# Hybrid trunk: weight sums in place, a second decay tile, and unit inputs added on VectorE

## The chip, the cores and the metric

The kernel runs on one core of one Trainium2 chip. The metric is the device time of one execution in microseconds (us). Engines are named as the profile does: PE is TensorE's matmul, PEld its weight load, DVE is VectorE, ACT ScalarE, POOL GpSimd, and SP the SyncE queue, from which nearly all DMA transfers are issued.

## The reference

One layer over 2048 positions with 1024 channels in f32. A normalised input goes through one projection `w_in`; its columns feed a short gated convolution (group A) and a chunked state-space scan (group B). The two results are concatenated, projected by `w_out` and added to `x`; then follow a norm, a squared-ReLU MLP, and a last norm. Cut to its skeleton:

```python
h = rmsnorm(x, norm_mix_w)
u_b, u_c, u_h, z, xbc, dt_raw = split(h @ w_in)
y_a = u_b * causal_dwconv(u_c * u_h, short_conv_w)
y_b = ssd_mixer(z, xbc, dt_raw, ...)        # conv, silu, chunked scan, gate, norm
x = x + concatenate([y_a, y_b]) @ w_out
h = rmsnorm(x, norm_mlp_w)
x = x + square(relu(h @ w_up)) @ w_down
out = rmsnorm(x, final_norm_w)
```

In the scan, each chunk of a head has a decay matrix: the exponential of differences of running sums, with what lies above the diagonal set to zero. It weighs the scores of the chunk before they are multiplied with its inputs.

## The kernel before

Positions are held in four blocks of 512 (`TB`), channels on the 128 partitions. Every large product is made of f32 operands that are split in two: `hi` is a cast to fp32r on ScalarE and `lo` the rest, subtracted on VectorE (`split_w`, L101 to L105, for weights, with lines L103 and L104; `settle`, L390 and L391, for inputs). A product is then three matmuls of 128x128 by 128x512: hi by hi, hi by lo, lo by hi (L315 to L317, in `chain`).

Most of the large products use seven products in place of eight. The chain `b11, t1, t2, b21, t3, b22, t4` takes a pair of weight blocks `r0`, `r1` and two sums of them, `s12` and `s34`. `combine` makes these: it yields the split of `r0`, then of `s12`, then of `s34`, then of half of `r1`. Raw weights lie in three `wraw` buffers, the sums in `sumtile`, a pool `us` of two buffers. With `kept` the sums are also stored and read back by the second half. With `kept == "none"`, which pair 3 of the output projection sets (`sums_d["o4"]`), all sums are made first and nothing is stored, and its first split comes one step later.

The output projection (`Output`) works in two parts. Eight pairs (`pair`) treat group A's half of `w_out` by the seven products, and store partial sums to DRAM (`x1_d`). The scan's second part, chunks 20 to 31, runs beside them: `hook` steps the generator `scan.run`, whose chunk is a `front` (transposes, decay, copies of the chunk's input) and a `back` (state, outputs, gate). The tiles of the second part come from the pool `sp2` with one buffer each, but for `bc` with two. The decay tile `dec` holds 8 rows of running sums, broadcast by a DMA (L1380). ScalarE makes eight Relus in place of it (L1431), one cast for the states (`xtok`, L1432) and one exponential (L1433); VectorE masks it (L1439), and the matmuls `yd` (L1456) read it. `run` issues the loads of chunk n + 1 (`load`) after the second step of `back(n)`.

Then come 32 plain units (`unit`, n = 32 to 63) for group B's half of `w_out`. A unit is 24 matmuls (L1687 to L1689) into one PSUM bank. The bank is first filled by ScalarE with the block of `x` that the residual adds: `seed`, L1658, from the tile `xr`, which has one buffer and is loaded by L1665. The first matmul of a unit then accumulates onto the seed. VectorE adds the partial sum `xt` (three buffers, load L1653) to the bank (the evict, L1691), the result goes back to `x1_d` (store, L1692), and for the first half of the positions its square is taken for the MLP's norm (`square`). Banks are taken in turn from `k0`, `k1` and `k2`. So the bank of unit n is the bank of unit n + 3, and the load of `xt` of unit n + 3 waits for the store of unit n.

From unit 48 on, the MLP's first input places are made beside the units: `prepare(0, ...)` scales the stored rows (`first`, `stay`, `nb`; L439), sums them (`sub`, L234), and `settle` splits them (L390, L391). `sums_of(0, 0)` makes the first weights of `w_up` ahead. After unit 63, PE goes into the MLP (`half`), whose `prepare(1, ...)` squares the stored rows of the second half of the positions (loads `lx`, squares L418).

The order of the instructions on each engine is not that of the Python text. A scheduler places them by its own estimates of when operands are there, within what the pools, the semaphores and `tc.issue_after` allow; the text sets what may precede what, and which buffer waits for which.

## Time and profile before

| what | value |
|---|---|
| median of 3 timed runs | 2607.75 us (2606.67 to 2608.23) |
| profiled execution, its own time | 2605.26 us |
| span of its instructions | 2603.5 us |
| mean granted TensorE clock | 0.996 |
| PE busy | 2570.4 us (99%), 12027 matmuls |
| PEld busy | 2110.9 us (81%) |
| DVE busy | 1928.4 us (74%), 2619 instructions |
| ACT busy | 1438.0 us (55%), 2199 instructions |
| POOL busy | 74.7 us (3%) |
| DMA | 552.84 MB, mean 212 GB/s |

The 2605.26 us are the device time of the one execution that the profile shows; the span is the part of it between its first and last instruction. All times of single instructions come from this execution, counted from the span's start. Matmuls are pipelined: each is shown with 0.39 us, but the next starts 0.23 us after it, so the rows of PE overlap. In a row of a timeline, the numbers are start and duration, and the bracket at its end is the time in which the engine stood idle before it and what released it. In a list of waits stand the total, the count and the longest.

The parts of the span that the change concerns, all read from the timeline: the second part of the scan runs from about 985 us, its last chunk ends at about 1235; unit 32 starts at 1156, unit 48 at 1263, unit 63 at 1347, and the MLP's first product at 1353.

### The profile page before, as it was taken

The numbers are of one execution on the slowest core, as the hardware profiler recorded it, in microseconds if no ns is written. First come the engines' busy times: TensorE is split into PE (matmuls) and PEld (weight loads), VectorE is DVE, ScalarE is ACT, GpSimd is POOL, SyncE is SP. The second block draws the span as 40 slices with busy tenths as digits, with TensorE's granted clock in tenths as the row PEclk, the third lists the DMA queues.
The fourth block names the chain that finished last, engine by engine and source line by source line (L and its number), as shares of the span: only waits on it lengthen the run. The fifth ranks groups of instructions, "written<-read, shape, count | busy, mean of one in ns | idle before, by whom it ended". The sixth has DMA issues, their size and how long they took to land.

```text
span 2603.5 us, 33796 instructions
## 1 busy us (share of the span) xinstructions
PE 2570.4 (99%) x12027; PEld 2110.9 (81%) x12027; DVE 1928.4 (74%) x2619; ACT 1438.0 (55%) x2199; POOL 74.7 (3%) x99
## 2 busy tenths in 40 slices
PE   9999999999999999999999999999999999999998
PEld 7888878788888887778878888888888888888887
DVE  7877776878787777888777765644448887888985
ACT  6554345876576666766346555655556444444443
POOL 2110010000000000000000000000000000000001
PEclk9999999999999999999999999999999999999999
DMA  4555665766655567878876785865557664665762
GB/s 168 181 190 185 220 237 184 234 194 197 195 179 186 171 231 250 261 232 278 261 234 230 270 316 221 294 211 194 194 190 260 187 183 150 213 211 179 239 208 76
DMA packets 258856, 552.84 MB, mean 212 GB/s; under 512 B 26976, under 2 KB 94336, under 8 KB 258688
## 3 DMA queue, kind: packets, MB, share of 16 engines
q1 hardware_dynamic: 258112, 549.78, 63.1%
q8 instruction: 94, 1.54, 0.2%
q10 hardware_dynamic: 576, 0.92, 0.1%
q14 instruction: 74, 0.61, 0.1%
HBM read 364.20 MB, written 186.40 MB: 211 GB/s over the span
## 4 chain that ended last, share of the span: by engine, by line
PE 78%; DVE 7%; DMA 7%; ACT 4%; issue 3%; SPq 0%; POOL 0%; POOLq 0%; DVEq 0%; ACTq 0%
PE px L315 14%; PE px L316 14%; PE px L317 14%; PE py L315 7%; PE py L316 7%; PE py L317 7%; PE pw L315 3%; PE pw L317 3%; PE pw L316 3%; DMA dec<-rd_d 1%; DMA xr<-x 1%; DVE ul L391 1%; PE yd L1456 1%; ACT dec L1431 1%; DVE wlo L104 1%
## 5 line engine op out<-in xcount | busy, mean ns | idle before, releaser
L315 PE MATMUL px<-uh,whi 128*128 128x512 f32 x1800 | 706.4, 393 | 8.8 <-DVE xt L1691 4.1
L317 PE MATMUL px<-uh,wlo 128*128 128x512 f32 x1800 | 702.4, 390 | 0.0
L316 PE MATMUL px<-ul,whi 128*128 128x512 f32 x1800 | 701.9, 390 | 0.0
L315 PEld LDWEIGHTS px<-uh,whi 128*128 128x128 f32 x1800 | 338.3, 188 | 86.9 <-DVE xt L1691 4.5
L317 PEld LDWEIGHTS px<-uh,wlo 128*128 128x128 f32 x1800 | 338.3, 188 | 73.1 <-issue 2.2
L316 PEld LDWEIGHTS px<-ul,whi 128*128 128x128 f32 x1800 | 338.4, 188 | 69.0 <-issue 0.3
L104 DVE TENSOR_TENSOR wlo<-wraw,whi 128x512 fp32r<-128x512 f32 (+1 forms) x213 | 217.3, 1020 | 201.3 <-ACT whi L103 199.0
L315 PE MATMUL py<-uh,whi 128*128 128x512 f32 x900 | 352.4, 392 | 1.6 <-ACT facc L1625 1.1
L317 PE MATMUL py<-uh,wlo 128*128 128x512 f32 x900 | 350.9, 390 | 0.0
L316 PE MATMUL py<-ul,whi 128*128 128x512 f32 x900 | 350.5, 389 | 0.0
L103 ACT CAST whi<-s 128x1024 fp32r<-128x1024 f32 x226 | 236.3, 1046 | 192.3 <-PE py L316 88.1
L104 DVE TENSOR_TENSOR wlo<-s,whi 128x1024 fp32r<-128x1024 f32 x226 | 275.2, 1218 | 88.8 <-ACT whi L103 87.7
L103 ACT CAST whi<-wraw 128x1024 fp32r<-128x1024 f32 (+1 forms) x214 | 190.2, 889 | 254.4 <-PE px L316 208.5
L315 PEld LDWEIGHTS py<-uh,whi 128*128 128x128 f32 x900 | 169.0, 188 | 40.2 <-issue 2.1
L316 PEld LDWEIGHTS py<-ul,whi 128*128 128x128 f32 x900 | 169.0, 188 | 35.3 <-issue 0.8
L317 PEld LDWEIGHTS py<-uh,wlo 128*128 128x128 f32 x900 | 169.0, 188 | 35.3 <-issue 0.2
L315 PE MATMUL pw<-uh,whi 128*128 128x512 f32 x450 | 176.3, 392 | 0.0
L317 PE MATMUL pw<-uh,wlo 128*128 128x512 f32 x450 | 175.3, 390 | 0.0
L316 PE MATMUL pw<-ul,whi 128*128 128x512 f32 x450 | 175.1, 389 | 0.0
L391 DVE TENSOR_TENSOR ul<-rh,uh 128x1024 fp32r<-128x1024 f32 (+1 forms) x128 | 138.7, 1088 | 32.1 <-ACT uh L390 32.1
L390 ACT CAST uh<-rh 128x1024 fp32r<-128x1024 f32 (+1 forms) x128 | 119.8, 941 | 73.0 <-PE py L317 59.4
L322 ACT COPY pw<-px 128x512 f32<-128x512 f32 x115 | 65.8, 573 | 125.9 <-PE px L317 125.5
(272 smaller groups left out, 3686.8 us busy)
## 6 DMA issues: line engine op xcount, KB each, us to landing
hid_d<-e SPq DMA_DIRECT2D x96, 512.0 KB, 3.3
rh<-hid_d SPq DMA_DIRECT2D x96, 512.0 KB, 4.6
wraw<-w_in SPq DMA_DIRECT2D x68, 512.0 KB, 4.2
wraw<-w_down SPq DMA_DIRECT2D x104, 256.0 KB, 3.5
wraw<-w_up SPq DMA_DIRECT2D x48, 512.0 KB, 3.7
dec<-rd_d SPq DMA_DIRECT2D x32, 512.0 KB, 5.3
wraw<-w_out SPq DMA_DIRECT2D x32, 512.0 KB, 5.3
sums_d<-s SPq DMA_DIRECT2D x32, 512.0 KB, 5.0
```

The costliest lines, as they stand in the source:

```text
L103: nc.scalar.copy(hi, raw)
L104: split["last"] = eng.tensor_tensor(out=lo, in0=raw, in1=hi.bitcast(F32), op=ALU.subtract)
L315: nc.tensor.matmul(p, hi, h[0], start=not seeded and k == 0, stop=False, **kw)
L316: nc.tensor.matmul(p, hi, h[1], start=False, stop=False, **kw)
L317: nc.tensor.matmul(p, lo, h[0], start=False, stop=(k == len(g) - 1), **kw)
L322: nc.scalar.copy(pm[gi]["w"], pm[gi]["x"])
L390: nc.scalar.copy(p[i][0], t)
L391: nc.vector.tensor_tensor(out=p[i][1], in0=t, in1=p[i][0].bitcast(F32), op=ALU.subtract)
L1431: nc.scalar.activation(dec[:, i], dec[:, i], AF.Relu, bias=t["a"][:, i : i + 1], scale=-1.0)
L1456: nc.tensor.matmul(yd[(i % 2) * 64 : (i % 2) * 64 + 64, (i // 2) * L : (i // 2 + 1) * L], byhead(t["xdt"])[:, i, :], t["dec"][:, i % 2 * 4 ...
```

## The change

It has four parts.

*Sums in place.* `Seven.inplace`: with it, `combine` writes `s34` over the raw tile `r0`, which has been split by then, instead of into a tile of `us`. It is set for the output projection and for the MLP's first weights (until unit 63 is done). The pool `us` of the output projection falls to one buffer; the tile `rn` of `norm` shares it. Pair 3 loses its path of its own (`"none"`) and takes the normal order of splits.

*Decay tiles in two buffers.* `sp2` is opened with two buffers, and all its tiles but `dec` (and `bc`) are held to one. `run` issues the loads of chunk n + 1 one step earlier. On SyncE, this is the load of a `dec` tile near the end of the pairs (`y`: the gate; `xd`, `bc`, `eb`: other tiles of the chunk; `rn`, `ry`: for scaling group B's rows; `x1`: partial sums). Before:

```order
L1401 DMA y_10254<-sz_d1_108 128x4x128
L1508 DMA rn_10379<-rn_d1_0_113 128x512
L1378 DMA xd_10329<-xs_d1_106 128x4x128
L1508 DMA rn_10379<-rn_d1_1_114 128x512
L98 DMA wraw_10426<-w_out 128x1024
L1665 DMA xr_10422<-x 128x512
L1653 DMA xt_10363<-x1_d0_77 128x512
L98 DMA wraw_10503<-w_out 128x1024
L1562 DMA ry_10371<-yn_d0_109 128x2x512
L1627 DMA x1_d2_79<-facc_10274 128x512
L1380 DMA dec_10331<-rd_d3_126 128x1024
```

and now:

```order
L1379 DMA bc_10300<-xs_d1_106 128x128
L1397 DMA eb_10132<-rd_d3_126 64x512 x2
L1379 DMA bc_10300<-xs_d1_106 128x128
L1383 DMA dec_10305<-rd_d3_126 128x1024
L1633 DMA x1_d3_80<-xt_10004 128x512
L1477 DMA yn_d1_110<-y_10049 128x4x128
L98 DMA wraw_10176<-w_out 128x1024
L1633 DMA x1_d2_79<-facc_10152 128x512
L1404 DMA y_10247<-sz_d1_108 128x4x128
L1381 DMA xd_10303<-xs_d1_106 128x4x128
L1678 DMA xr_10415<-x 128x512
```

The load has moved from behind the chunk's `y`, `xd`, `rn`, two raw weights and others to ahead of them, right behind `bc`.

*Seeds up to unit 47.* The tiles `xr` of units 35 to 47 lie in places of `ul3` that are not in use then, with four buffers, and for units 34 to 45 `seed(n)` also issues the load of unit n + 2. The copies on ScalarE stay.

*Units 48 to 63 without seeds.* ScalarE copies nothing. The unit's first matmul starts the bank, and VectorE adds `xr` to `xt` (L1695 of the changed kernel) right after the evict of the unit before, before its own evict (L1712 there). `xr` comes from a pool `late` with two buffers, loaded two units ahead. On VectorE this is the stretch around the evict of unit 57 (`wlo`: split of a weight; `ul`: split of an input; `s12`, `s34`: sums of the first `w_up` pair). Before, from a sum for the MLP's input to that evict, the last row:

```order
L234 TENSOR_TENSOR nb_11867<-nb_11868,first_11866 128x512
L391 TENSOR_TENSOR ul2_11929<-nb_11868,uh2_11928 128x1024
L234 TENSOR_TENSOR nb_11869<-nb_11867 128x512
L1691 TENSOR_TENSOR xt_11748<-pm_11768,xt_11748 128x512
L104 TENSOR_TENSOR wlo_11847<-wraw_11844,whi_11846 128x1024
L391 TENSOR_TENSOR ul3_11933<-nb_11869,uh3_11932 128x512
L269 TENSOR_TENSOR s12_12057<-wraw_11971 128x512
L234 TENSOR_TENSOR s34_12095<-wraw_11969,wraw_11971 128x512
L234 TENSOR_TENSOR s12_12057<-s12_12057,wraw_11969 128x512
L234 TENSOR_TENSOR s34_12095<-wraw_11969,s12_12057 128x512
L1691 TENSOR_TENSOR xt_11794<-pm_11808,xt_11794 128x512
```

and now, the adds of units 57 and 58 among them, the evict of unit 57 in the seventh row:

```order
L1695 TENSOR_TENSOR xt_11786<-xt_11786,xr_11749 128x512
L442 SCALAR_TENSOR_TENSOR nb_11859<-nb_11859,cv_169,facc_10478 128x512
L236 TENSOR_TENSOR first_11858<-nb_11861,first_11858 128x512
L236 TENSOR_TENSOR nb_11860<-nb_11860,nb_11861 128x512
L236 TENSOR_TENSOR nb_11859<-nb_11860,first_11858 128x512
L271 TENSOR_TENSOR s12_12049<-wraw_11963 128x512
L1712 TENSOR_TENSOR xt_11786<-pm_11803,xt_11786 128x512
L1695 TENSOR_TENSOR xt_11834<-xt_11834,xr_11789 128x512
L236 TENSOR_TENSOR nb_11861<-nb_11859 128x512
L393 TENSOR_TENSOR ul2_11921<-nb_11860,uh2_11920 128x1024
L393 TENSOR_TENSOR ul3_11925<-nb_11861,uh3_11924 128x512
L236 TENSOR_TENSOR s12_12049<-s12_12049,wraw_11961 128x512
```

Two splits of inputs and four sums that stood ahead of the evict of unit 57 now stand behind it, and adds stand ahead of and behind it. The end of the units, from the evict of unit 62 to that of unit 63, before:

```order
L1691 TENSOR_TENSOR xt_12009<-pm_12023,xt_12009 128x512
L104 TENSOR_TENSOR wlo_12100<-s34_12095,whi_12099 128x1024
L269 TENSOR_TENSOR s12_12233<-wraw_12175 128x512
L391 TENSOR_TENSOR ul1_12130<-stay_11585,uh1_12129 128x1024
L234 TENSOR_TENSOR s12_12233<-s12_12233,wraw_12173 128x512
L391 TENSOR_TENSOR ul1_12134<-stay_11679,uh1_12133 128x1024
L391 TENSOR_TENSOR ul1_12138<-stay_11773,uh1_12137 128x1024
L1691 TENSOR_TENSOR xt_12065<-pm_12079,xt_12065 128x512
```

and now:

```order
L1712 TENSOR_TENSOR xt_12001<-pm_12018,xt_12001 128x512
L1695 TENSOR_TENSOR xt_12057<-xt_12057,xr_12004 128x512
L104 TENSOR_TENSOR wlo_12091<-wraw_11961,whi_12090 128x1024
L393 TENSOR_TENSOR ul1_12122<-stay_11577,uh1_12121 128x1024
L393 TENSOR_TENSOR ul1_12126<-stay_11671,uh1_12125 128x1024
L393 TENSOR_TENSOR ul1_12130<-stay_11765,uh1_12129 128x1024
L1712 TENSOR_TENSOR xt_12057<-pm_12072,xt_12057 128x512
```

Between the two evicts stands the add of unit 63, and the two sums of the next weights are gone from there. PE's order is the same as before throughout.

*Loads for the second half.* `prepare(1, ...)` may issue its `lx` loads only behind the store of unit 63.

The diff, cut to its core:

```diff
         def combine(self, r0, r1, kept=None):
...
-            s34 = self.sumtile("s34")[:, 0 : 2 * w]
+            s34 = r0 if self.inplace else self.sumtile("s34")[:, 0 : 2 * w]
...
-        def prepare(self, h, src, base, accs=None):
+        def prepare(self, h, src, base, accs=None, begin=None):
...
-                                nc.sync.dma_start(ts[-1], src[h * NBB + bb][:, j : j + 2])
+                                with tc.issue_after(begin.ins) if begin else nullcontext():
+                                    nc.sync.dma_start(ts[-1], src[h * NBB + bb][:, j : j + 2])
...
-            t["dec"] = self.tile([HG, L], "dec")
+            t["dec"] = self.tile([HG, L], "dec", self.bufs)
...
                 next(back)
+                if self.bufs > 1:
+                    self.load(n + 1)
                 yield
                 next(back)
-                self.load(n + 1)
+                if self.bufs == 1:
+                    self.load(n + 1)
...
             if p == 3:
                 proj.new = [{} for _ in range(4)]
-                sums_d["o4"] = "none"
...
                 pm = self.pm[n] = psum("mm", "pm")
-                nc.scalar.copy(pm, self.res.pop(n))
-                self.origin(n + 1)
+                if n < 48:
+                    nc.scalar.copy(pm, self.res.pop(n))
+                if n < 48:
+                    self.origin(n + 1)
+                if 33 < n < 46:
+                    self.origin(n + 2)
...
-                t = self.res[n] = self.small("xr")
+                if n < 35 or n == 48:
+                    t = self.small("xr")
+                elif n > 48:
+                    t = self.late.tile([P, TB], F32, tag="xr", name="xr", bufs=2)
+                else:
+                    t = uh.tile([P, TB], F32, tag="ul3", name="xr", bufs=4)
+                self.res[n] = t
                 nc.sync.dma_start(t, x[b, :, d])
...
+            fresh = n >= 48
+            if fresh:
+                with tc.issue_after(self.evicted.ins):
+                    nc.vector.tensor_tensor(out=self.xt[n], in0=self.xt[n], in1=self.res.pop(n), op=ALU.add)
+                if n == 48:
+                    self.origin(49)
+                self.origin(n + 2)
...
+                nc.tensor.matmul(pm, w, hi, start=fresh and j == 0, stop=False, **kw)
...
-            proj.sumtile = lambda name: os.tile([P, 1024], F32, tag="us", name=name, bufs=2)
-            scan.open(c2, "sp2", 1)
+            proj.sumtile = lambda name: os.tile([P, 1024], F32, tag="us", name=name, bufs=1)
+            scan.open(c2, "sp2", 2)
...
-        ws = mlp.half(0, ws, mlp.prepare(1, x1_d, C_NMLP))
+        ws = mlp.half(0, ws, mlp.prepare(1, x1_d, C_NMLP, begin=proj_out.stored))
```

More of the change, by code (lines that the diff above doesn't have):

```diff
@@ L216, in trunk @@
     class Seven:
+        inplace = False
         def __init__(self):
@@ L1369, in load @@
             if (g, c) == (0, 0) or n == self.begin:
-                dd = self.tile([4, NC * 16], "dd")
+                dd = self.tile([4, NC * 16], "dd", 1)
                 nc.sync.dma_start(dd, dt_d[b])
@@ L1399, in load_gate @@
             b, g, c, h, ts, r0 = self.place(n)
-            y = self.got[n]["y"] = self.tile([4, L], "y")
+            y = self.got[n]["y"] = self.tile([4, L], "y", 1)
             nc.sync.dma_start(y, sz_d[h][:, 4 * g : 4 * g + 4, ts])
@@ L1586, in open @@
             proj.fresh = self.raw
+            proj.inplace = True
         def raw(self, name):
@@ L1635, in after @@
                     proj.got = proj.fetch(0)
-                if p == 3:
-                    if name == "t1":
-                        next(ahead)
-                    if name != "b11":
-                        proj.refresh(name)
+                if p == 3 and name != "b11":
+                    proj.refresh(name)
                 hook(7 * p + n)
@@ L1686, in unit @@
                 w, v = whi[:, k, :], wlo[:, k, :]
-                nc.tensor.matmul(pm, w, hi, start=False, stop=False, skip_group_check=True)
-                nc.tensor.matmul(pm, w, lo, start=False, stop=False, skip_group_check=True)
-                nc.tensor.matmul(pm, v, hi, start=False, stop=(j == KD - 1), skip_group_check=True)
+                kw = dict(skip_group_check=not fresh)
+                nc.tensor.matmul(pm, w, hi, start=fresh and j == 0, stop=False, **kw)
+                nc.tensor.matmul(pm, w, lo, start=False, stop=False, **kw)
+                nc.tensor.matmul(pm, v, hi, start=False, stop=(j == KD - 1), **kw)
             t = self.xt.pop(n)
-            nc.vector.tensor_tensor(out=t, in0=pm, in1=t, op=ALU.add)
-            nc.sync.dma_start(x1_d[b][:, d], t)
+            self.evicted = nc.vector.tensor_tensor(out=t, in0=pm, in1=t, op=ALU.add)
+            self.stored = nc.sync.dma_start(x1_d[b][:, d], t)
             if i and b < NBB:
@@ L1774, in trunk @@
         mlp.up = proj_out.xp
-        mlp.us = c4.enter_context(tc.tile_pool(name="us", bufs=1, side="right", reuse_waits="tile"))
+        mlp.inplace = True
         c7 = c4.enter_context(ExitStack())
+        proj_out.late = c7.enter_context(tc.tile_pool(name="late", bufs=1, side="right", reuse_waits="tile"))
+        mlp.sumtile = lambda name: proj_out.late.tile([P, 1024], F32, tag="us", name=name, bufs=1)
         stay = c7.enter_context(tc.tile_pool(name="stay", bufs=1, side="right", reuse_waits="tile"))
@@ L1799, in trunk @@
         c7.close()
+        mlp.us = c4.enter_context(tc.tile_pool(name="us", bufs=1, side="right", reuse_waits="tile"))
+        mlp.inplace = False
+        del mlp.sumtile
     turns.update(mm=itertools.cycle(("k0", "k1", "k2", "k4")), mw=itertools.cycle(("k3", "k5")), fresh=("k3", "k5"))
```

4 lines of the change are left out of this document (2 added, 2 removed).

## The prediction

> **What bounds the kernel now.** I read the page first, then the busy time by stretch, then TensorE's waits in the stretch that the change touches, then the timelines around the longest of them. PE's instructions stand in the same order in both kernels, and the other queues in nearly the same up to about 985 us, so the time before that I take as given. The stretch from 985 to 1365 us (second scan part beside the w_out pairs, its end beside the units, the units alone, the start of the MLP); the columns are busy time and instructions of PE, PEld, DVE, ACT and POOL, then PE's clock, the DMA share and GB/s:
>
> ```profile
> 985.00:1365.00 380.00, 365.38 (x1815) 296.70 (x1814) 298.57 (x420) 221.10 (x400) 0.00 (x0) 1.00 0.79 252
> ```
>
> PE is busy for 365.4 of 380 us, and its matmul count does not change: the change can win no more than the 14.6 us in which PE stands still there, and little beside. VectorE is the second engine, at 79%. TensorE's waits from 855 to 1375 us, total, times, longest:
>
> ```profile
> PE px L315 <- DVE xt L1691: 4.1, 1, 4.1
> PE pn L1486 <- ACT xtok L1416: 2.5, 1, 2.5
> PE pm L1687 <- ACT pm L1658: 2.5, 4, 1.3
> PE st L118 <- ACT xtok L1432: 2.4, 2, 1.5
> PE py L315 <- ACT facc L1625: 1.1, 1, 1.1
> PE px L315 <- DVE xt L1622: 0.9, 1, 0.9
> PE st L119 <- DVE stmp L1434: 0.9, 2, 0.5
> PE ptx L1411 <- DMA xd<-xs_d: 0.7, 1, 0.7
> ```
>
> The releasers are ACT and DVE, but these are late themselves. ScalarE's own waits from 855 to 1240 us say for what:
>
> ```profile
> ACT pm L1658 <- DMA xr<-x: 24.3, 7, 8.6
> ...
> ACT dec L1431 <- DMA dec<-rd_d: 16.6, 10, 5.3
> ```
>
> Two loads into single buffers, the unit seeds xr and the decay rows dec, hold ScalarE's queue, and PE pays behind it. The places on PE that the sum uses:
>
> ```profile
> 1005.48 0.50 PE L118 MATMUL st<-xtok,btok 128*128 128x512 f32 x1 [1.50 <-ACT xtok L1432]
> ...
> 1159.27 0.43 PE L1486 MATMUL pn<-ssq,ones_r 128*32 128x128 f32 x8 [2.52 <-ACT xtok L1416]
> ...
> 1206.50 0.50 PE L1687 MATMUL pm<-uh,whi 128*128 128x512 f32 x1 [1.32 <-ACT pm L1658]
> ...
> 1330.18 0.50 PE L1687 MATMUL pm<-uh,whi 128*128 128x512 f32 x1 [0.42 <-ACT pm L1658]
> ...
> 1359.03 0.69 PE L315 MATMUL px<-uh,whi 128*128 128x512 f32 x1 [4.06 <-DVE xt L1691]
> ```
>
> **Decay tiles in two buffers.** SyncE's load and ScalarE's next Relu at the costlier chunk (the later SyncE rows are used below):
>
> ```profile
> 1147.14 0.33 SPq L1380 DMA_DIRECT2D dec<-rd_d  x1
> ...
> 1309.31 0.32 SPq L1653 DMA_DIRECT2D xt<-x_d  x1
> ...
> 1348.23 0.32 SPq L1653 DMA_DIRECT2D xt<-x_d  x1
> ```
>
> ```profile
> 1154.05 1.29 ACT L1431 ACTIVATE dec<-dec,dd 128x128 f32<-128x128 f32 x4 [5.29 <-DMA dec<-rd_d]
> ```
>
> The load goes out only when the yd matmuls have read the last tile, and ScalarE gets it nearly 7 us later; the copies that PE waits for are queued behind the eight Relus. With a second buffer the load stands 12 rows earlier on SyncE at this place, ahead of gate, xd and rn loads. On it hang 1.5 us of PE at 1005, 2.5 at 1159, and the longer of the two waits on L1434, 0.5, which comes by the same chain through VectorE: 4.5 in all. Next late are xd and eb, which keep one buffer. Bounds of what they take back: 0, if they keep ahead, and all 4.5, if they land as late as dec did. The trace has xd as PE's last wait once, for 0.7; I take 1.0, near that row, so 3.5 net.
>
> **Seeds of units 33 to 47.** Their xr tiles now lie in unused places and load up to two units ahead. The 1.3 us at 1206 are the longest wait on L1658, and ScalarE's backlog there comes from its stops on xr, the longest of 8.6 us. Bounds 0 and 1.3; I take 1.3.
>
> **Units 48 to 63: copies go, adds come.** Sixteen seed copies leave ScalarE, and with them the other three waits on L1658, 2.5 - 1.3 = 1.2 us, since the first matmul of these units starts the bank itself. Sixteen adds xt += xr come to VectorE, each right behind the evict of the unit before. The nearest row is the evict, the same addition with one operand in PSUM:
>
> ```profile
> L1691 DVE TENSOR_TENSOR xt<-pm,xt 128x512 f32<-128x512 f32 x18 | 12.3, 686 | 5.0 <-DMA xt<-x_d 5.0
> ```
>
> ```profile
> 1278.63 3.35 DVE L189 RECIPROCAL facc<-facc 128x512 f32<-128x512 f32 x1 [3.34 <-ACT facc L188]
> ...
> 1313.76 0.71 DVE L1691 TENSOR_TENSOR xt<-pm,xt 128x512 f32<-128x512 f32 x1
> ...
> 1318.79 0.75 DVE L439 SCALAR_TENSOR_TENSOR nb<-nb,cv,facc 128x512 f32<-128x512 f32 x1 [2.52 <-DMA nb<-x_d]
> ...
> 1326.66 1.28 DVE L1691 TENSOR_TENSOR xt<-pm,xt 128x512 f32<-128x512 f32 x2
> ...
> 1358.29 0.69 DVE L1691 TENSOR_TENSOR xt<-pm,xt 128x512 f32<-128x512 f32 x1
> ```
>
> Two in a row take 1.28 us, so each puts back what follows by 0.60: 16 x 0.60 = 9.6 us of VectorE. Is there room? A unit's bank is needed again three units later. The first evict at 1326.66 is unit 57's; it ends at 1327.3, and unit 60, which takes that bank, began at 1330.2: slack 2.8 us. Eight adds (50 to 57) put evict 57 back by 4.8. Against that the first reciprocal no longer waits 3.34: its sqrt stood on ScalarE behind a seed copy that waited for xr, and now follows the sum of squares directly. And the order moves one split of 1024, one of 512 and four sums of 512 elements from ahead of evict 57 to behind it, about 1.1 + 0.6 + 4 x 0.6 = 4.1. So it moves by 4.8 - 3.3 - 4.1 = -2.6 us, and by up to 2.5 more if the idle time before 1318.79 fills. Under that cover the adds cost nothing; without it (neither gap closes, the order as before) evict 57 would be 4.8 later, and PE would lose 4.8 - 2.8 = 2.0.
>
> The add also waits for its xt and xr. Queued behind it on VectorE are the scalings and sums for the MLP's input and the evict of its own unit; ScalarE's casts of nb, the store, and PE by its bank wait for those. On SyncE the xr load two units on waits for the add, with the unit's store behind it. The sixteen xt loads of L1653:
>
> ```profile
> DMA to landing us min/median/max: 2.8/4.8/6.3
> ```
>
> The load at 1309.31 is unit 56's, the tightest of units 51 to 58; evict 55, behind which add 56 stands, began 4.45 us later, at 1313.76. Add 56 would thus wait between 0 and 1.9 us, 0.4 by the median. With evicts earlier by a like amount the stores are too, so I count this as zero.
>
> One rule bears on these loads: the Trainium skill, "DMA: Bandwidth & Descriptors", section "Anatomy of one DMA — SWDGE (gpsimd) path", fits a transfer as about 2.0 us plus its bytes at 436 GB/s (on another issue path than this), which I turn into an estimate of 2.6 us for the 256 KB of xt. The trace disagrees, with a median of 4.8 at this DMA share; by the page no add would wait, the residual of the next part would be nil, and the sum 0.8 better.
>
> **Into the MLP.** The longest stall, seen on ScalarE:
>
> ```profile
> 1345.20 0.59 ACT L1658 COPY pm<-xr 128x512 f32<-128x512 f32 x1 [2.53 <-DMA xr<-x]
> ```
>
> PE's 4.1 us at 1359 wait for unit 63's evict at 1358.29. That stood behind a VectorE queue that began late, since ScalarE's casts of the MLP's first places came after this copy, held 2.5 us for xr. The copy is gone, and so are the squares for half 1, whose lx loads wait for the last store now. New is add 63: from the landing of xt 63 the add, one split and three subtractions stand ahead of evict 63, 0.6 + 4 x 1.1 = 5.0 us. With its load at 1348.23, landing at 1351.0 to 1354.5, evict 63 would start at 1356.0 to 1359.5, hardly better than 1358.29. But that load follows, by stores and three buffers, from evict 60 and that from evict 57. Evict 60 is the one that waited 5.0 for xt (the L1691 row), and evict 57 moves 2.6 to 5.1 us up; with 3 us on the chain evict 63 starts at 1353.0 to 1356.5. PE began to wait at 1359.0 - 4.1 = 1354.9. So with evict and restart of 0.75 the residual lies between 0 and 2.4, more (3.3) if the chain gains only 2; I take 0.8. Gain 3.3.
>
> **In one sentence each.** With s34 in the first raw tile and one us buffer, a raw tile is held until its last split, and the next pair's second load starts a few us later; a pair's 84 matmuls outlast these loads several times, so it costs 0 (up to 1 us if a first product comes late). Pair 3 without its extra path: PE's waits on L1625 and L1622, 1.1 + 0.9 = 2.0, hang on a backlog of casts that stays; between 0 and 2.0, I take 0.4. The squares for half 1 have all of half 0 to finish in, cost 0.
>
> **The sum.** 3.5 + 1.3 + 1.2 + 3.3 + 0.4 = 9.7 us won. The profiled execution took 2605.26 us (span 2603.5), 2.5 under the median of the three timed runs, 2607.75, whose lowest is 2606.67. It would go to 2595.6, and on the median's basis 2607.75 - 9.7 = 2598.0. With each term at its good end (4.5 + 1.3 + 1.2 + 4.1 + 2.0 = 13.1) it is 2594.6; with each at its bad end (0 + 0 + 1.2 + 0.8 + 0 - 1.0 = 1.0) 2606.8.
>
> **Rivals.** *The add chain keeps the last stall.* Add 63 waits for its load as reckoned with nothing earlier, and PE still stands 4 us before the MLP. For it: the same three xt buffers and the same way from store to load. Against it: three causes of the lateness go. Gain 9.7 - 3.3 = 6.4, 2601.3; chance 0.13. *xd or eb takes the place of dec.* For it: a DMA share of 0.79 and one buffer each; against it the single wait of 0.7. Gain 9.7 - 3.5 = 6.2, 2601.5; chance 0.13. *The adds are paid in full.* If VectorE sets the end of the units, 9.6 come back and 0.1 is left: 2607.6, no change; against it stand the 5.0, 3.3 and 2.5 us in which VectorE idles; chance 0.06. The Trainium skill, "VectorE: DVE Perf Modes", section "Rules for kernel authors", speaks for this one: it advises to keep the count of chained operations low, and the change raises it by 16. *Slower.* The adds wait for xt at each of units 50 to 57, w on average. With the slack of 2.8 + 2.6 = 5.4 used up, PE pays 8w - 5.4; the kernel loses when that exceeds 9.7, w over 1.9, and by over 0.2% from w = 2.6. At 2.8 it is 17.0, so 7.3 slower, 2615.1. The tightest load bounds its wait at 1.9, against this; chance 0.06.
>
> **Numbers.** Forecast 0.62, rivals as given. About 0.2%, 5.2 us, is what a measurement of this kernel can tell from no change: faster means under 2602.5, which takes the forecast and some 0.16 of the first two rivals, 0.78; the rest of them and the third make 0.16; slower 0.06. The range runs from the good end, 2594.5, to 2604.5, the first two rivals and 3 us for their terms at bad ends; what lies beyond, the last two rivals and tails, is about 0.15.
>
> **What would show it.** In the profile after: no wait of ScalarE for dec over 1 us from chunk 21 on, no PE idle at st and pn; no wait of PE on L1658 after unit 33; evict 57 at least 4 us ahead of unit 60's start; PE idle before the MLP's second product under 2 us. I am wrong if the adds wait over 2 us each for xt, if xd takes the place of dec, or if new PE idle stands in the pairs, on a weight split that comes late.

## The result and the profile after

In its first runs the change gained more than forecast. The changed kernel took 2595.07 us as the median of four runs (2589.88 to 2597.05) beside 2607.99 for the kernel before (2606.67 to 2609.54), a ratio of 0.9947 [0.993, 0.9964]: 12.9 us by the medians, 9.4 to 18.3 by the interval, against a forecast gain of 9.7. On two other chips the same pair gave 0.9956 [0.9943, 0.9969] and 0.9965 [0.9952, 0.9978], or 11.8 and 9.0 us. Over all runs on record, 65 of the kernel before and 15 of the changed one, the medians are 2607.75 and 2597.06 us, 10.7 us apart, so the forecast of 9.7 is not far from the gain.

The profiled execution took 2595.14 us (span 2593.4, clock 0.997). The stretch from 985 to 1365 us, columns as before:

```profile
985.00:1365.00 380.00, 373.89 (x1864) 306.17 (x1863) 311.96 (x439) 218.87 (x388) 0.00 (x0) 1.00 0.79 255
```

PE stands still for 6.1 us there, where it stood still for 14.6. Its waits from 855 to 1375 us:

```profile
PE px L317 <- DVE xt L1628: 2.3, 1, 2.3
PE ptx L1414 <- DMA xd<-xs_d: 2.2, 1, 2.2
PE px L317 <- ACT s L807: 1.0, 1, 1.0
PE pm L1708 <- ACT uh L1583: 0.9, 1, 0.9
PE st L118 <- ACT xtok L1435: 0.7, 1, 0.7
PE px L317 <- DVE eb L810: 0.5, 1, 0.5
PE st L119 <- DVE stmp L1437: 0.3, 1, 0.3
```

The waits on the unit seeds, on `pn` and on unit 63's evict are gone. Two that were short have grown: the one for xd in place of 0.7, and the one in pair 3 (L1628) in place of 0.9. ScalarE still waits for dec from 855 to 1240 us:

```profile
ACT dec L1434 <- DMA dec<-rd_d: 13.8, 5, 4.2
```

The second buffer took 2.8 of 16.6 us from it, and the longest is 4.2 in place of 5.3. The two grown waits on PE:

```profile
1010.15 0.33 PE L1414 MATMUL ptx<-ident,xd 128*128 128x128 f32 x1 [2.16 <-DMA xd<-xs_d]
...
1062.88 0.50 PE L317 MATMUL px<-uh,whi 128*128 128x512 f32 x1 [2.32 <-DVE xt L1628]
...
1064.31 0.63 PE L319 MATMUL px<-uh,wlo 128*128 128x512 f32 x1
1064.73 0.63 PE L317 MATMUL px<-uh,whi 128*128 128x512 f32 x1
```

At 1010 xd is the last to land, which is the rival from the prediction, at this one place. And dec is late still: ScalarE waits for it 4.1 us at 1172 and 3.2 at 1214, where the prediction had no wait over 1 us from chunk 21 on as a sign of being right. Behind the wait at 1063 something else shows. From 1064.3 matmuls last 0.63 us and start 0.42 apart, where 0.23 is usual. The same stretch as a window, with the clock in the third column from the end:

```profile
1063.90:1067.20 3.30, 3.30 (x9) 2.61 (x8) 2.65 (x4) 3.27 (x4) 0.00 (x0) 0.51 0.89 290
```

The clock was granted at half over these 3.3 us. The kernel before has the same behind its longest stall, the 4.06 us at 1359:

```profile
1359.00:1362.40 3.40, 3.37 (x8) 2.72 (x9) 3.40 (x5) 0.00 (x0) 0.00 (x0) 0.53 0.56 141
```

```profile
1359.52 0.63 PE L316 MATMUL px<-ul,whi 128*128 128x512 f32 x1
1359.95 0.63 PE L317 MATMUL px<-uh,wlo 128*128 128x512 f32 x1
...
1362.79 0.40 PE L315 MATMUL px<-uh,whi 128*128 128x512 f32 x1
1363.03 0.40 PE L316 MATMUL px<-ul,whi 128*128 128x512 f32 x1
```

Eight matmuls at 0.43 us in place of 0.23 are 1.6 us that no idle time shows, and the prediction put them at nothing. In the profile after, the way into the MLP is clean, with PE busy throughout and the clock at 1.00:

```profile
1345.00:1360.00 15.00, 15.00 (x67) 12.09 (x66) 12.63 (x16) 9.52 (x11) 0.00 (x0) 1.00 0.68 228
```

**Place by place.** All but 197 of PE's 12027 matmuls stand at the same place of its order in both profiles, so each can be paired with itself. The 197 lie between the marks of the table (at 1002 to 1017, 1060 to 1084, 1159 to 1180 and 1354 to 1367 us). There PE's order did change, against what was said of it ahead of the result: ahead of `pn`, for one, stand five matmuls of unit 32 where two stood before. The difference of a matmul's two starts says how far ahead the changed kernel is there; the growth from one mark to the next (before's time) is the gain of that stretch. Three profiles of the changed kernel (the two others are the controls f0 after and f0 again below), in us:

| stretch | what lies there | forecast | after | f0 after | f0 again |
|---|---|---|---|---|---|
| 980–1056 | st at 1005, xd | 0.5 | 0.4 | -1.6 | -0.8 |
| 1056–1085 | pair 3 | 0.4 | -1.7 | -0.8 | 0.4 |
| 1085–1140 | st at 1104 | 0.5 | 1.2 | 1.2 | 1.2 |
| 1140–1200 | pn at 1159 | 2.5 | 1.4 | 1.6 | 1.7 |
| 1200–1255 | seeds of units 33 to 47 | 1.3 | 1.6 | 0.4 | -0.6 |
| 1255–1345 | units 48 to 63 | 1.2 | 2.1 | 2.1 | 2.1 |
| 1345–1400 | into the MLP | 3.3 | 5.8 | 5.7 | 5.9 |
| sum | | 9.7 | 10.8 | 8.6 | 9.7 |

The three sums average 9.7, the forecast, by errors that cancel: the last two rows gave 3.4 more than forecast, the first five 3.4 less. At 980 us, ahead of which little is changed, the same comparison already reads between -6.8 and +0.7 us in the profiles of the changed kernel and its variants, so a difference of two whole executions says less than these rows.

### The profile page after: what moved, and what is told of

It reads as the page before. It is cut to its first block, busy times and chain, and to the rows that moved or that the text cites. A ratio compares the mean times of both kernels' runs of the same rounds, so it can differ in the third digit from the quotient of the medians.

```text
span 2593.4 us, 33806 instructions
## 1 busy us (share of the span) xinstructions
PE 2567.1 (99%) x12027; PEld 2109.9 (81%) x12027; DVE 1937.1 (75%) x2635; ACT 1430.7 (55%) x2183; POOL 76.5 (3%) x99
## 4 chain that ended last, share of the span: by engine, by line
PE 81%; DMA 6%; DVE 6%; ACT 4%; issue 3%; POOL 0%; SPq 0%; POOLq 0%; DVEq 0%; ACTq 0%
PE px L317 13%; PE px L319 13%; PE px L318 13%; PE py L317 7%; PE py L318 7%; PE py L319 7%; PE pw L317 3%; PE pw L319 3%; PE pw L318 3%; PE pm L1708 2%; DMA dec<-rd_d 2%; PE pm L1709 2%; PE pm L1710 2%; DVE ul L393 1%; ACT dec L1434 1%
## 5 line engine op out<-in xcount | busy, mean ns | idle before, releaser
L104 DVE TENSOR_TENSOR wlo<-wraw,whi 128x512 fp32r<-128x512 f32 (+1 forms) x221 | 226.4, 1025 | 199.5 <-ACT whi L103 195.5
L103 ACT CAST whi<-wraw 128x1024 fp32r<-128x1024 f32 (+1 forms) x222 | 198.8, 896 | 275.8 <-PE px L318 216.5
L103 ACT CAST whi<-s 128x1024 fp32r<-128x1024 f32 x218 | 228.2, 1047 | 195.9 <-PE py L318 85.5
L104 DVE TENSOR_TENSOR wlo<-s,whi 128x1024 fp32r<-128x1024 f32 x218 | 265.0, 1216 | 83.2 <-ACT whi L103 82.2
```

Of the source, the lines that this page charges most:

```text
L103: nc.scalar.copy(hi, raw)
L104: split["last"] = eng.tensor_tensor(out=lo, in0=raw, in1=hi.bitcast(F32), op=ALU.subtract)
```

## The experiments

Each expectation carries its own theories: where it speaks of A and B, A is the theory held then and B the rival. All edits are to the changed kernel but where said. Ratios are against the kernel before on the same chip.

**Is the gain in the scan the second decay buffer's?** (e1)

```diff
-            scan.open(c2, "sp2", 2)
+            scan.open(c2, "sp2", 1)
```

> The changed kernel with the scan's second pool back at one buffer for dec, its loads one step later as before; all other parts of the change stay. Theory A (second dec buffer only trades one wait for another, dec for xd): the wait of 2.2 us on xd at 1010 goes, dec waits of 1.5, 0.5 and 2.5 us come back, so the kernel is 1 to 3 us slower than the changed one (2595 on the changed kernel's median), and the waits before the MLP stay gone. Rival B (the second buffer carries the gain): slower by 4.5 us or more. Rival C (it is worth nothing): within 1 us, with PE's idle time from 985 to 1200 us unchanged.

Measured: 2597.49 us against 2607.66, 0.9963 [0.9951, 0.9975], inside the spread of the changed kernel's own three ratios. By places it is told apart: the wait at `pn` is back.

```profile
1160.98 0.32 PE L1489 MATMUL pn<-ssq,ones_r 128*32 128x128 f32 x4 [2.03 <-ACT xtok L1419]
```

At 1010 there is no wait for xd. So the buffer does remove waits for dec. The rows from 980 to 1200 us of the table add up to -0.5 us in this profile, and to 1.3, 0.4 and 2.4 in those of the changed kernel: by one profile of e1, the buffer is worth about 2 us and not 3.5. That it makes xd late isn't shown, for with one dec buffer PE waits for xd as well: here 1.9 us at 988.83, and 2.35 in e5 below.

**Do the adds on VectorE give anything?** (e2) Here units 48 to 63 are seeded by ScalarE again; the two xr buffers and loads two units ahead stay.

```diff
-                if n < 48:
-                    nc.scalar.copy(pm, self.res.pop(n))
+                nc.scalar.copy(pm, self.res.pop(n))
...
-            fresh = n >= 48
-            if fresh:
-                with tc.issue_after(self.evicted.ins):
-                    nc.vector.tensor_tensor(out=self.xt[n], in0=self.xt[n], in1=self.res.pop(n), op=ALU.add)
+            fresh = False
+            if n >= 48:
```

> The changed kernel, but units 48 to 63 are seeded by ScalarE copies again, from the same two xr buffers loaded two units ahead; no adds on VectorE. Theory A (what held ScalarE was the load of xr into a single buffer, not the copy): ScalarE's waits on xr shrink, evict 63 comes in time, PE idle before the MLP under 1 us, time within 1.5 us of the changed kernel. Rival B (the copies themselves in ScalarE's queue delay the casts and PE's unit starts): PE idle of 3 us or more before the MLP, a drop of PE's clock behind it, 4 to 7 us slower than the changed kernel.

Measured: 2593.25 us, 0.9952 [0.9939, 0.9964]. The units and the way into the MLP, as two windows:

```profile
1255.00:1345.00 90.00, 90.00 (x398) 74.53 (x398) 70.42 (x86) 36.27 (x48) 0.00 (x0) 1.00 0.71 233
1345.00:1360.00 15.00, 15.00 (x66) 12.05 (x66) 12.21 (x17) 8.84 (x12) 0.00 (x0) 1.00 0.78 268
```

PE is busy for all 105 us without one add. So the adds are not what ended the long stall; nor do they show a cost.

**Does a second xd buffer recover the rest?** (e4)

```diff
-            return self.tile([512], "stmp", 3)
+            return self.tile([512], "stmp", 4 - self.bufs)
...
-            t["xd"] = self.tile([4, L], "xd", 1)
+            t["xd"] = self.tile([4, L], "xd", self.bufs)
```

> The changed kernel with two buffers for xd too; to make room for it, the scan's second part has two buffers for stmp in place of three. Theory A (xd took the place of dec as the late load): PE's wait on xd at about 1010 us, 2.2 us, goes and nothing else comes, 1.5 to 2.2 us faster than the changed kernel. Rival B (eb, or stmp with a buffer less, is late next): the idle time comes back within the same chunk on another releaser, within 1 us of the changed kernel or slower.

Measured: 2598.28 us, 0.9958 [0.9947, 0.997]. The wait for xd is gone, and others stand in its place, a new one on `stmp` among them, which paid for the room with a buffer, and the kernel is no faster:

```profile
998.52 0.49 PE L118 MATMUL st<-xtok,btok 128*128 128x512 f32 x1 [1.80 <-ACT xtok L1435]
...
1196.12 0.80 PE L119 MATMUL st<-stmp,btok 128*128 128x512 f32 x1 [2.49 <-DVE stmp L1437]
```

**Is pair 3's longer wait due to its lost path?** (e5) The path "none" of pair 3 comes back with its second sum buffer; dec goes to one buffer for the room.

```diff
+                sums_d["o4"] = "none"
...
-                if p == 3 and name != "b11":
-                    proj.refresh(name)
+                if p == 3:
+                    if name == "t1":
+                        next(ahead)
+                    if name != "b11":
+                        proj.refresh(name)
...
-            proj.sumtile = lambda name: os.tile([P, 1024], F32, tag="us", name=name, bufs=1)
-            scan.open(c2, "sp2", 2)
+            proj.sumtile = lambda name: os.tile([P, 1024], F32, tag="us", name=name, bufs=2)
+            scan.open(c2, "sp2", 1)
```

> e1_dec1 (one dec buffer) and, besides, pair 3's own path of before (all sums first, first split one step later), for which the pool us has two buffers again; sums in place elsewhere stay. Theory A (the wait of 2.3 us of PE on pair 3's evict comes from the normal order of sums and splits): this wait falls under 1.2 us, and the kernel is 1 to 2 us faster than e1_dec1. Rival B (the backlog of input casts in pair 3 is the cause in either order): waits of 2 us or more remain in pair 3, within 0.7 us of e1_dec1.

Measured: 2598.78 us, 0.9968 [0.9955, 0.9981]. Pair 3 still waits, and so does the scan for xd:

```profile
1007.57 1.11 PE L1414 MATMUL ptx<-ident,xd 128*128 128x128 f32 x4 [2.35 <-DMA xd<-xs_d]
...
1070.65 0.50 PE L317 MATMUL px<-uh,whi 128*128 128x512 f32 x1 [1.90 <-DVE xt L1629]
...
1169.96 0.32 PE L1489 MATMUL pn<-ssq,ones_r 128*32 128x128 f32 x4 [2.13 <-ACT xtok L1419]
```

So the lost path isn't the cause. The last row, the `pn` wait that one dec buffer brings back, drew half clock behind it, where before's 2.52 us and e1's 2.03 us at the same place did not:

```profile
1171.40:1174.80 3.40, 3.40 (x10) 2.64 (x9) 3.40 (x6) 3.36 (x5) 0.00 (x0) 0.51 0.45 143
```

**Is the slow start of the MLP the clock, or its operands?** Two kernels put dummy matmuls of 128x512 behind unit 63 of the kernel before, to shorten the idle time: 17 of them (e6 warm17), and 5 (e6 warm5, with 5 in place of 17).

```diff
+        for i in range(17):
+            if i == 0:
+                warm = psum("k5", "warm")
+            ins = nc.tensor.matmul(warm, ones_r, ones_r.unsqueeze(1).to_broadcast([P, 4, P]), start=(i == 0), stop=(i == 17 - 1))
```

> The kernel before with 17 extra matmuls of 128x512 of ones into an unused bank, right behind unit 63; the MLP's first product then starts with px. Theory A (PE's clock fell because PE stood still for 4 us): with the stall shortened to some 2.5 us, the first px matmuls behind it follow each other at 0.23 us, not 0.43, and the granted clock stays at 1.0 from 1359 to 1362. Rival B (these matmuls are slow for what they read, or by the load of other engines and DMA): they still start 0.43 us apart.

> As the run with 17 extra matmuls, but 5 of them, so that PE still stands still for 3.5 us or more before px. Theory A: the matmuls behind the stall start 0.43 us apart for some 3 us, as in the kernel before. Rival B: the same, so that this run only shows, beside the other, that extra matmuls alone change nothing.

Measured, one run each: 2613.27 and 2616.76 us, against 2607.36 for the kernel before. With 17:

```profile
1361.97 0.47 PE L315 MATMUL px<-uh,whi 128*128 128x512 f32 x1 [2.07 <-DVE xt L1691]
1362.28 0.39 PE L316 MATMUL px<-ul,whi 128*128 128x512 f32 x1
...
1363.42 0.63 PE L315 MATMUL px<-uh,whi 128*128 128x512 f32 x1
```

With 5:

```profile
1368.10 0.80 PE L315 MATMUL px<-uh,whi 128*128 128x512 f32 x1 [4.47 <-DVE xt L1691]
1368.69 0.63 PE L316 MATMUL px<-ul,whi 128*128 128x512 f32 x1
```

With 17 the first matmuls on these operands run at full rate, so it isn't the operands. But 1.45 us later the clock falls all the same, behind a stall of only 2.07 us, so the 2.5 us of the expectation were wrong too. With 5 the stall grew no shorter. Both kernels were also scheduled in another order, so their times say nothing.

**Does the hold on the `lx` loads matter?** (e7)

```diff
-        ws = mlp.half(0, ws, mlp.prepare(1, x1_d, C_NMLP, begin=proj_out.stored))
+        ws = mlp.half(0, ws, mlp.prepare(1, x1_d, C_NMLP))
```

> The changed kernel without the hold on the lx loads: squares for half 1 may again stand among the units. Theory A (the hold matters little, since the copies were what waited): within 1 us of the changed kernel and PE idle before the MLP under 1 us. Rival B (the squares on ScalarE, waiting for lx, delay the casts as they did): PE idle before the MLP of 1.5 us or more, 1.5 to 5 us slower.

Measured: 2594.02 us, 0.9944 [0.9928, 0.9959]. PE has no idle time there without the hold either:

```profile
1345.00:1360.00 15.00, 15.00 (x67) 12.09 (x66) 14.66 (x20) 8.86 (x11) 0.00 (x0) 1.00 0.60 199
```

**How much room has VectorE, and where does it end?** (e9) Three operations per unit in place of one add.

```diff
-                    nc.vector.tensor_tensor(out=self.xt[n], in0=self.xt[n], in1=self.res.pop(n), op=ALU.add)
+                    xr = self.res.pop(n)
+                    for op in (ALU.add, ALU.subtract, ALU.add):
+                        nc.vector.tensor_tensor(out=self.xt[n], in0=self.xt[n], in1=xr, op=op)
```

> The changed kernel with three VectorE instructions in place of each add (add, subtract, add of the same xr), 32 more of 0.6 us in units 48 to 63. Theory A (VectorE has little room left there, a slack of some 5 us before PE's banks are late): of 19 us more work most exceeds the slack, PE waits on evicts, 5 to 15 us slower. Rival B (VectorE's idle time takes it all): within 1.5 us of the changed kernel.

Measured: 2607.81 us, 0.9993 [0.9981, 1.0004]. Of 32 more operations at 0.60 us, 19.2 us, PE lost nothing in the units (the table's 2.1 stays). It lost 7 in the next stretch (-1.3 for 5.8). The evict of unit 63 comes late, PE's order there is another one, with the product `pw` ahead of `px`, and `pw` waits for a split of VectorE; the clock falls beside it:

```profile
1359.75 0.80 PE L318 MATMUL pw<-ul,whi 128*128 128x512 f32 x1 [2.21 <-DVE ul L393]
```

```profile
1360.00:1364.00 4.00, 3.82 (x8) 2.09 (x9) 4.00 (x6) 0.00 (x0) 0.00 (x0) 0.50 0.28 109
```

So PE's banks coming late, the way of the prediction's rival "slower", isn't how VectorE's work comes to count here. It comes to count at the MLP's first splits, which stand behind the units' work.

**Is the second xr buffer what matters?** Once with the seeds on ScalarE (e2's edit and this one, f1), once with the adds (this one alone, f3):

```diff
-                    t = self.late.tile([P, TB], F32, tag="xr", name="xr", bufs=2)
+                    t = self.late.tile([P, TB], F32, tag="xr", name="xr", bufs=1)
```

> e2_seeds (ScalarE seeds units 48 to 63, no adds) with one xr buffer in place of two. Theory A (the single xr buffer was the cause of the stall before the MLP): ScalarE's waits on xr come back, 10 us or more from unit 48 on, evict 63 is late, PE stands still for 2 to 4 us before the MLP and, where that is over some 2 us, its clock may be halved behind it for 3 us; 3 to 6 us slower than e2_seeds. Rival B (the order of the sums made in place, or their moving behind the units, took the stall away): PE idle before the MLP stays under 1 us, within 1.5 us of e2_seeds.

> The changed kernel (adds on VectorE) with one xr buffer in place of two for units 49 to 63. Theory A (adds need the load early as the copies do): VectorE waits on xr in most units, evicts fall behind, PE loses 2 us or more in units 50 to 63 or before the MLP. Rival B (the add, a unit before its evict, leaves the load enough time even from one buffer): within 1.5 us of the changed kernel, no PE idle over 0.5 us in the units.

Measured: f1 2599.34 us, 0.9957 [0.9942, 0.9973]; f3 2603.27, 0.9977 [0.9966, 0.9987]. PE in f1:

```profile
1309.65 0.50 PE L1705 MATMUL pm<-uh,whi 128*128 128x512 f32 x1 [0.95 <-ACT pm L1661]
...
1357.07 0.50 PE L317 MATMUL px<-uh,whi 128*128 128x512 f32 x1 [1.15 <-DVE xt L1709]
```

PE in f3, with 13 matmuls at half clock behind it:

```profile
1355.77 0.79 PE L317 MATMUL px<-uh,whi 128*128 128x512 f32 x1 [3.46 <-DVE xt L1712]
```

With one buffer the adds bring nearly the whole stall back, and the kernel is 5.4 us slower than the changed one beside it (2597.91, f0 after below). With the seeds part of it comes back (0.95 and 0.3 us in the units and 1.15 behind them), 1.4 us by the medians; the 1.15 us lie between theory A's 2 to 4 and rival B's under 1. The adds need the second buffer more than the seeds do.

**What does it take to keep the gain?** (h1) f1's kernel (no adds, one xr buffer) without the hold on `lx` (e7's edit): in units 48 to 63 the inputs come as in the kernel before.

> f1_one (seeds by ScalarE, one xr buffer) without the hold on the lx loads, so that three squares for half 1 stand among the last seed copies again, as in the kernel before. Theory A (squares and seeds together make the wait of 4 us; either alone makes less): PE stands still for 3 us or more before the MLP's first px product and runs at half clock behind it. Rival B (the hold does nothing here either; the order of the sums made the difference): the wait stays within 1 us of f1_one's 1.2.

Measured: 2598.18 us, 0.9951 [0.9931, 0.9971]. ScalarE waits 25.3 us for xr from 1255 to 1360 us, and still PE has no idle time in the units or into the MLP (the table's last rows read 2.1 and 5.9). The end of the units on ScalarE and VectorE in h1:

```profile
1338.96 0.59 ACT L1661 COPY pm<-xr 128x512 f32<-128x512 f32 x1 [2.67 <-DMA xr<-x]
1339.49 3.89 ACT L392 CAST uh<-first 128x1024 fp32r<-128x1024 f32 x4
...
1348.64 1.06 ACT L392 CAST uh<-stay 128x1024 fp32r<-128x1024 f32 x1 [0.30 <-PE pm L1707]
```

```profile
1345.71 0.68 DVE L1709 TENSOR_TENSOR xt<-pm,xt 128x512 f32<-128x512 f32 x1
1346.31 1.22 DVE L104 TENSOR_TENSOR wlo<-wraw,whi 128x1024 fp32r<-128x1024 f32 x1
1347.44 3.52 DVE L393 TENSOR_TENSOR ul<-stay,uh 128x1024 fp32r<-128x1024 f32 x3
1350.87 0.68 DVE L1709 TENSOR_TENSOR xt<-pm,xt 128x512 f32<-128x512 f32 x1
```

And in the kernel before:

```profile
1345.72 3.89 ACT L390 CAST uh<-first 128x1024 fp32r<-128x1024 f32 x4
```

```profile
1351.95 0.69 DVE L1691 TENSOR_TENSOR xt<-pm,xt 128x512 f32<-128x512 f32 x1
...
1353.68 0.69 DVE L269 TENSOR_TENSOR s<-wraw 128x512 f32<-128x512 f32 x1
...
1358.29 0.69 DVE L1691 TENSOR_TENSOR xt<-pm,xt 128x512 f32<-128x512 f32 x1
```

From evict 62 to evict 63 it is 5.2 us in h1 and 6.3 before, two sums less. To compare the rest, PE's own lead is taken off: h1's PE is 3.0 us ahead at 1345, its casts of `first` 6.2 (1339.49 against 1345.72), so the casts are 3.3 ahead of PE's progress. The same for the other kernels, with the evict of unit 63:

| kernel | input of units 48 to 63 | casts ahead | evict 63 ahead | PE's stall |
|---|---|---|---|---|
| before | seeds, one xr buffer | 0 | 0 | 4.06 |
| f1 | seeds, one | 1.9 | 3.1 | 1.15 |
| h1 | seeds, one, `lx` not held | 3.3 | 4.5 | none |
| e7 | adds, two, `lx` not held | 5.2 | 4.5 | none |
| e2 | seeds, two | 7.7 | 4.5 | none |
| after | adds, two | 7.7 | 4.5 | none |
| f3 | adds, one | 7.7 | 0.8 | 3.46 |

More than 4.5 isn't to be had, for then the casts of `stay` wait for unit 63's own matmuls (the last ScalarE row of h1). With seeds the evict's lead is the casts' and the two sums': 1.9 + 1.2 = 3.1 in f1, and 3.3 + 1.2 = 4.5 in h1, just enough. Two xr buffers bring the casts 7.7 ahead whether they feed seeds or adds, where `lx` is held. So the gain there has two sources: earlier casts, for which a second xr buffer gives room and one is at the edge, and the sums' new places. Why the casts are ahead with one buffer at all goes back past evict 60, which waits for PE in f1 and h1 and waited 5.0 for xt before; that the order of the sums alone does this wasn't tried on the kernel before.

**A version with all of it?** (f2) e2's kernel with two xd buffers, and the xr tiles of units 32 to 34 and 48 in unused places.

```diff
-            t["xd"] = self.tile([4, L], "xd", 1)
+            t["xd"] = self.tile([4, L], "xd", self.bufs)
...
-                if n < 35 or n == 48:
-                    t = self.small("xr")
+                if n < 35:
+                    t = uh.tile([P, 2, TB], F32, tag="ul0", name="xr", bufs=4)[:, 0]
```

> e2_seeds with xd in two buffers and stmp still in three; room for it comes from xr of units 32 to 34, which lie in places of ul0 that are unused then, and of unit 48 in ul3. Theory A (xd is the wait that took dec's place, and e4_xd2 lost it again to stmp): no PE wait on xd or stmp over 1 us from chunk 21 on, 1 to 2 us less in the scan's stage than e2_seeds, the rest the same; about 2591. Rival B (another load or VectorE's queue is late next): no gain over e2_seeds within 1 us.

Measured: 2599.28 us, 0.9964 [0.9951, 0.9977], not the 2591 expected and 1.4 us over the changed kernel beside it. No wait for xd is left at 1010; pair 3 waits longer instead:

```profile
1063.46 0.50 PE L317 MATMUL px<-uh,whi 128*128 128x512 f32 x1 [3.42 <-DVE xt L1628]
```

**Can pair 3's wait be taken away?** (g1) e2's kernel with pair 3's input splits one product later, so that the evict L1628 stands ahead of three splits on VectorE. g2 is the same on f2.

```diff
-                if p == 3 and name != "b11":
-                    proj.refresh(name)
+                if p == 3:
+                    i = {"t2": 0, "t3": 1, "t4": 2}.get(name)
+                    if i is not None:
+                        proj.settle(proj.new, i, proj.got)
+                        proj.got = proj.fetch(i + 1)
+                    if name == "t4":
+                        proj.settle(proj.new, 3, proj.got)
```

> e2_seeds with pair 3's input splits asked for one product later each, so that on VectorE the evict at about 1057 us stands ahead of three of them and no longer behind. Theory A (this order makes PE's wait on the evict in pair 3, and the clock's fall behind it where it comes): the wait on L1628 of 0.6 to 3.4 us goes under 0.5, 1 to 3 us faster than e2_seeds. Rival B (the splits only come late in turn and hold the next pair's first product): the wait moves to a first product of pair 4, within 1 us of e2_seeds.

> g1_late with xd in two buffers as in f2_best. Theory A (f2_best lost xd's gain in pair 3): PE's waits on xd and on the evict of pair 3 are both under 0.7 us, 1 to 2 us faster than g1_late. Rival B (the scan's next load or VectorE's queue takes it again): within 1 us of g1_late or slower.

Measured: g1 2592.82 us, 0.9946 [0.9934, 0.9959]; g2 2597.39, 0.9969 [0.9956, 0.9981]. PE's waits in g1 from 985 to 1420 us:

```profile
PE ptx L1414 <- DMA xd<-xs_d: 1.9, 2, 1.6
PE px L317 <- ACT pw L324: 1.8, 1, 1.8
...
PE px L317 <- DVE xt L1628: 0.5, 1, 0.5
```

The wait on L1628 fell to 0.5, and part of it came back two products later on ScalarE's `pw`. Still all five runs of g1 (2588.06 to 2595.02) lie under all five of the changed kernel beside it (2596.78 to 2597.90), 4.6 us by the medians, and 4.0 under e2's. That it beats e2 isn't settled, for e2's first runs on that chip had a median of 2593.25, and in the places pair 3 gives -0.2 us in g1 against -0.5 and -2.9 in the two profiles of e2; the edit also changed PE's order there. In g2 L1628 waits 2.9 again: the second xd buffer gains nothing here either.

**Controls.** The changed kernel beside f1, f2 and f3 (f0 after), and beside g1 and g2 (f0 again), with e2 there too (e2 again).

> The changed kernel itself, once more, beside the others on the same chip: by its first runs 2592 to 2597 in the median. Theory A (a stall of some 2 us halves PE's clock behind it only in some executions): the profile of this execution differs from the first one by 1 to 3 us in the stretch up to 1100 us, with or without the half clock behind the wait in pair 3. Rival B (executions are alike): the same stalls and the same half clock at the same places within 0.3 us.

> The changed kernel on the same chip as the three others: 10 to 13 us under the kernel before, since the end of the units alone gives 6 and the rest 3 to 6.

> e2_seeds again, beside the changed kernel on the same chip. Theory A (the second xr buffer is what counts, copy or add the same): medians within 2 us of each other. Rival B (the adds do better than copies): 2 us or more slower than the changed kernel.

Measured: 2597.91 us, 2597.43 (9.0 under the kernel before, less than the 10 to 13 expected) and, for e2, 2596.84 with 0.9971 [0.9958, 0.9984] beside the changed kernel's 0.9965. So the adds show neither gain nor loss. The waits from 980 to 1140 us change from one execution of the same code to the next: xd cost PE 2.2 us in the profile after, 1.9 in two waits in f0 after, and 4.0 in two waits in f0 again, the longer of which is this,

```profile
1012.91 0.33 PE L1414 MATMUL ptx<-ident,xd 128*128 128x128 f32 x1 [3.21 <-DMA xd<-xs_d]
```

and pair 3's half clock stands in one of the three profiles. In f0 after the clock fell at 989.3, behind three waits of 0.85, 0.39 and 1.11 us that lie close together:

```profile
989.30:992.70 3.40, 3.17 (x12) 2.97 (x13) 0.95 (x3) 2.71 (x9) 0.00 (x0) 0.50 1.06 262
```

## Why the prediction was off, step by step

**Into the MLP: 3.3 forecast, 5.8 measured.** The mechanism was right and the size off. Casts that no longer stand behind a late xr, four sums moved behind evict 57 and two behind evict 63 bring the last evict forward; evict 57 is 7.7, 5.2 and 6.9 us ahead, with PE's lead at 1255 taken off, in the three profiles, against the 2.6 to 5.1 of the working. The step that failed is the price of the stall. By "the change can win no more than the 14.6 us in which PE stands still there, and little beside" the sum let this term be worth 4.1 us at its good end, its idle time, and put what comes behind a stall at nothing: behind the 4.06 us stood 3.4 us at half clock, 1.6 us more. And the residual of 0.8 didn't come, as the evict is as early as PE itself allows. The copies' going was not needed for that: e2 has them and the same 5.8, and h1 has them with one buffer.

**Units 48 to 63: 1.2 forecast, 2.1 measured.** The waits went, in e2 and h1 with the copies there too; in f1, where evict 57 is 1.6 us behind the kernel before, two came back. Each wait is idle time and a restart: before, three waits of 0.35 to 0.42 us put PE back by 0.63 to 0.70 each, and the sum counted the idle time alone. That the adds are covered was right, and e9 shows the cover: 9.6 us fit, 19.2 more do not.

**The scan: 3.5 forecast, about 2.1 measured** (rows 980, 1085 and 1140 of the table, 3.0, 1.2 and 2.1 us in the three profiles). Right were the direction and the price of `pn`: its wait went, came back with one buffer (e1), and at this place PE gained 2.7 us in each of the three profiles. What the stretch gave is less, 1.4 to 1.7, because a new wait, for a cast of ScalarE, follows 17 us later in all three, of 0.94, 0.71 and 0.64 us. That cast stands behind the Relus of the next `dec`, for which ScalarE waited 4.1 us here (3.8 in each of the two others). So dec's own lateness moved on by a chunk. In the profile after:

```profile
1172.25 2.46 ACT L1434 ACTIVATE dec<-dec,dd 128x128 f32<-128x128 f32 x8 [4.11 <-DMA dec<-rd_d]
1174.61 1.03 ACT L1583 CAST uh<-ry 128x1024 fp32r<-128x1024 f32 x1
```

```profile
1175.69 0.50 PE L1708 MATMUL pm<-uh,whi 128*128 128x512 f32 x1 [0.94 <-ACT uh L1583]
```

Too low was the price of xd: 1.0 put, and PE waited 1.9 to 4.0 us for it. The rival "xd takes the place of dec" is seen at 1010 and not at `pn`, and e1 and e5 wait for xd with one dec buffer too, so its cause is open. Removing xd's wait (e4, f2, g2) only shows the next in line, `xtok`, `stmp` or VectorE's evict in pair 3: a wait removed at one operand is found at another.

**Pair 3: 0.4 forecast, about -0.7 measured.** That the lost path makes its wait isn't borne out (e5). With the splits moved behind the evict (g1) the wait on L1628 falls to 0.5 us, and 1.8 on `pw` come in its place; how much of g1's time is due to that isn't shown.

**Seeds of units 33 to 47: 1.3 forecast, 1.6, 0.4 and -0.6 measured.** The wait on L1658 went, and at its place PE gained 1.5 us in all three. What the two later profiles lost again are waits of the scan beside the units, at 1210 and 1230 us, 0.8 us in f0 after and 1.7 in f0 again, mostly for `stmp` from VectorE. The first profile has none of these.

**The size.** By places the gain is the forecast's 9.7, with too much at the scan and too little at the MLP. The medians say 12.9, 11.8 and 9.0, and 10.7 over all runs. That the sum came out at 9.7 is luck, as its errors cancel. The profile of before that served as basis was one of its quick executions, 2605.26 us against a median of 2607.99, as noted then; the prediction took the gain to be the same for all. Part of this quickness lies ahead of the change: at 980 us the profile of before is ahead of 16 of the 18 others, by 1.4 us in the median. Another part, argued and not shown, may be that the 2.5 us stall at `pn` draws half clock in some executions of the kernel before and drew none in the one profiled.

## What to carry to other kernels

Price a stall of PE of some 1.9 us or more, or shorter ones close together, with what may stand behind it, 1.6 us at half clock here, and look at the granted clock just after it before calling PE's idle time the upper bound of a gain. When several edits meet at one place, leave each out in turn: here the adds that replaced the copies did nothing that a second buffer for the copies didn't do. Compare by pairing the same instruction in two traces, stretch by stretch and with the waiting engine's own lead taken off, since whole executions of one kernel differ by as much as most terms.

## What the runs showed of the hardware

The half clock was not expected. Over all 19 profiles, from 150 to 2570 us, it follows 15 of 22 stalls of PE of 1.87 to 2.52 us, one of six of 2.6 to 3.5, and both of 4.06 and 4.47. Of 114 stalls of 0.8 to 1.85 us, two have to do with a fall: the 0.85 and 1.11 us in f0 after, which stand close together. So the length of one stall does not decide it.

The traces' record of the granted clock says what does. In each profile the times between its changes are whole multiples of 3.413 us, so the clock is set in windows of that length, whose edges do not move with the stalls. Cut into these windows, the 19 profiles have 13447 at full clock. Half clock follows all 18 in which PE stands idle for 1.87 us or more, and one of the others, which have 1.82 or less: the 1.77 us in f0 after. A long stall that an edge cuts in two draws none: the 3.42 us of f2 lie as 1.60 and 1.82 in two windows. Half clock lasts one window, or two in three cases (e6 warm5, e9, f3), where PE stood still for 0.32 to 1.85 us in the first, against 0.23 at most in the others.

The Trainium skill, "TensorE: Matmul & The Clock Gate", section "Part 1: The HAM clock gate (the "warmup" mystery)", has the clock halved after an idle window of about 3.4 us, in windows that run on freely. The trace agrees with that length and with windows that run on freely. It disagrees with a window that is idle throughout: a little over half of one, 1.87 us, was enough in all 18 cases.
